# Forgetting attention: exponentials kept in PSUM, reciprocals spread over 128 partitions, four y buffers

## The chip, the cores and the metric

One core of one Trainium2 chip runs one encoder layer for a sequence of 1024 tokens of width 1024. The metric is the device time of one execution in microseconds, lower is better. A core has five engines that run side by side, each through its own instructions in order: PE (TensorE: matmuls; PEld is its weight load), DVE (VectorE), ACT (ScalarE), POOL (GpSimd) and SP (SyncE, which here only issues transfers). PE writes its results to PSUM, a small memory of eight banks of 128 partitions x 512 numbers; everything else lies in SBUF or in DRAM. POOL works on SBUF alone in this kernel.

## The reference, cut to what matters

```python
u = layer_norm(x) * (1 + scale) + shift             # scale, shift, gate from c
h = u @ w_in                                        # split in fq fk fv fg ff | sq sk sv sg
f_cum = cumsum(log_sigmoid(ff + b_f))
# forgetting attention, 8 heads of 64
s = (fq @ fk.T) / 8 + (f_cum[q] - f_cum[k])         # causal: -inf for k > q
y_fox = softmax(s) @ fv * silu(fg)
# stick-breaking attention, 8 heads of 64
y_sb = weights(sq, sk) @ sv * silu(sg)
out = layer_norm(alpha * x + gate * (concat(y_fox, y_sb) @ w_out)) * ln_g + ln_b
```

Every large product is computed in three matmuls: each operand is split in a rounded high part and a rest, and high x high, high x rest and rest x high are summed in PSUM.

## The kernel before, in words

The layer is cut in eight pairs of heads (p = 0 to 7): pairs 0 to 3 are the stick-breaking heads, pairs 4 to 7 the forgetting heads (hh = 0 to 7, p = 4 + hh // 2). The stages follow each other: the normalisation and first projections; the stick-breaking units (`units`, two turns behind them the transposes of `weights_turn`); then the forgetting attention; then the output projection, whose tiles of 128 tokens run in the order 6, 7, 4, 5, 2, 3, 0, 1.

**The order of the work.** PE's instructions stand in the order in which the program writes them (`manual_schedule`, L142 to L143). The other queues are ordered by a planner that simulates times, so a line lower in the program can run earlier there; a queue once ordered is run in order, and an instruction that waits holds what is behind it. The projections of later pairs are "fillers" (L1131): generators of small pieces, a piece about three matmuls of 512 columns, which the loops call between the attention's own work (`fill`, `share`).

**The loop of the forgetting attention** (L1235 to L1265) goes through 96 steps. A step is (head, query group g, key block kb): 128 keys against up to 512 queries. g=1 (the upper 512 queries) has eight key blocks, g=0 four; heads 0 to 5 run g=1 and then g=0, and the last two heads run (6,1), (7,1), (6,0), (7,0). In step n the program writes:

- `fox_scores` of step n (L615): two matmuls (L622, L623) put the scores of keys (partitions) by queries into T, a PSUM tile of two buffers; an additional row of the operands brings minus the row maximum. DVE adds the causal mask on the diagonal block (L625). ACT takes exp of T twice: into SBUF in full (L637, `raw`) and rounded (L638, the high part of `pt`). DVE subtracts the two for the rest (L639); POOL adds `raw` to the sum of the row (L643, in SBUF). After the last key block the sum's two halves of partitions are folded (ACT L646, DVE L647) and split in two parts (ACT L648, DVE L649);
- fillers, and for the groups six steps ahead (`AHEAD`) the maxima: `fox_max` (L588), a matmul into S (one buffer) and a DVE reduction (L600), four times; then `fox_row` (L605), a transpose by PE (L607), a copy by ACT and a transfer on SP's queue into the operand row;
- `fox_pv` of step n-2 (L653): the product with the values, in two PSUM accumulators, one for each half of 256 queries (L665). With a half's last key block, `att_joined` (L528) adds the accumulator's parts into a y buffer `ty` of SBUF (ACT L533, DVE L534 and L535), and the accumulator is free;
- four steps after a group's last score (`NORM_LAG`), `fox_norm` (L670): a matmul with ones spreads the row sum over all partitions into a T buffer (L675), DVE takes the reciprocal of 64 x 512 there (L676), multiplies the gate with it (L677), and `att_gated` (L538) multiplies y with the gate on POOL (L541) and stores it to `y_dr` on SP's queue (L549). For the last pair y stays in SBUF, in two parts (L546, L547).

`ty` has two buffers. From step 80 (`OUT_AT`) a piece of the output projection (L1039 to L1041) follows each step; `load_y` brings the stored y of a token tile back (L1016) and splits it on POOL (L1019, L1020).

Of the kernel before, what the change touches and what calls it, by code (L numbers as in the profile page):

```python
# [14 lines left out]
P = 128  # L15
# [13 lines left out]
def tile_hybrid_layer(  # L29
# [27 lines left out]
    def att_tile(name, dt=F32):  # L57
        return big("att", 6, name, dt)
# [10 lines left out]
    def t_tile(name):  # L69
        return ps.tile([P, 512], F32, tag="T", bufs=2, name=name)  # L70
# [42 lines left out]

    y_dr = dr.tile([NPAIR, P, SEQ], F32, tag="y_dr", name="y_dr")
    wo_dr = dr.tile([2, NPAIR, P, D], F32, tag="wo_dr", name="wo_dr")
    f_dr = dr.tile([3, 8, SEQ], F32, tag="f_dr", name="f_dr")

    def raw_tile(name):
# [404 lines left out]
        summed.append((acc, p, h, j))  # L523

    def att_sum(acc, p, h, j):
        att_gated(att_joined(acc, p, h, j), p, h, j)

    def att_joined(acc, p, h, j):  # L528
        r = slice(h * HD, h * HD + HD)
        o = slice((1 - h) * HD, (1 - h) * HD + HD)  # L530
        ty = sb.tile([P, 512], F32, tag="ty", bufs=2, name=f"ty_{p}_{h}_{j}")
        tm, yt = ty[:, :256], ty[:, 256:]
        nc.scalar.copy(tm[r, :], acc[o, :256])  # L533
        nc.vector.tensor_tensor(yt[r, :], acc[r, :256], tm[r, :], op=ALU.add)  # L534
        nc.vector.tensor_tensor(yt[r, :], acc[r, 256:], yt[r, :], op=ALU.add)  # L535
        return yt
# [17 lines left out]
    def fox_open():  # L554
        QA.append(att_tile("qa_0", F32R))
        wide = fx["wide"] = cp.tile([P, SEQ], BF16, tag="qz", name="wide")
        nc.gpsimd.memset(wide, 0.0)
        nc.gpsimd.affine_select(out=wide[:, SEQ - P:], in_=wide[:, SEQ - P:], pattern=[[-1, P]], base=0,
                                channel_multiplier=1, compare_op=ALU.is_ge, fill=MASKED)
        KA.append(big("kl", 2, "ka_0", F32R))  # L560
        for t in (QA[0], KA[0]):
            nc.gpsimd.memset(t.bitcast(F32)[HD:FK], 1.0)
        fox_load(0)
        tiles = [att_tile(f"fx_{n}") for n in range(3)]
        tiles.append(att_tile("fx_3", F32R))
        parts = [t[:, a:a + 512] for t in tiles for a in (0, 512)]
        fx["raw"], fx["fold"], fx["sum"], fx["hl"] = parts[:3], parts[3][:HD], parts[4:6], parts[6:]
        fx["row"] = parts[3][HD:HD + 4]

    def fox_more():  # L570
        QA.append(att_tile("qa_1", F32R))
# [33 lines left out]
    def fox_row(hh, g):  # L605
        t = s_tile(f"m_{hh}_{g}")[:4, 0, :P]
        nc.tensor.transpose(t, nms.pop((hh, g)), ident)  # L607
        row = fx["row"][:, nrow[0] % 4 * P:][:, :P].bitcast(F32R)
        nrow[0] += 1
        nc.scalar.copy(row, t)  # L610
        nc.sync.dma_start(QA[hh % 2].bitcast(F32)[FM:FK, g * 512:g * 512 + 512], row.bitcast(F32))

    pts, sums, nraw, nsum, hls = {}, {}, [0, 0], [0], {}

    def fox_scores(hh, g, kb):  # L615
        p, h = 4 + hh // 2, hh % 2
        qa, ka = QA[hh % 2], KA[hh % 2]
        q0 = max(0, kb * P - g * 512)
        ks = slice(kb * P, kb * P + P)
        qs = slice(g * 512 + q0, g * 512 + 512)  # L620
        T = t_tile(f"T_{hh}_{g}_{kb}")
        nc.tensor.matmul(T[:, q0:], ka[:FK, ks], qa[:FK, qs], start=True, stop=False)  # L622
        nc.tensor.matmul(T[:, q0:], kst[p][h][:, ks], qst[p][h][:, qs], start=False, stop=True)  # L623
        if kb >= 4 * g:
            nc.vector.tensor_tensor(T[:, q0:q0 + P], T[:, q0:q0 + P], causal, op=ALU.add)  # L625
        if nraw[0] % 2 == 0:
            fx["pt"] = pt_tile(f"pt_{nraw[0]}", F32R, [P, 2, 2, 512])
        pt = pts[hh, g, kb] = fx["pt"][:, nraw[0] % 2]
        nraw[0] += 1
        if kb == 0:  # L630
            raw = sums[hh, g] = fx["sum"][nsum[0] % 2]
            hls[hh, g] = fx["hl"][nsum[0] % 2]
            nsum[0] += 1
        else:
            raw = fx["raw"][nraw[1] % 3]
            nraw[1] += 1
        nc.scalar.activation(raw[:, q0:], T[:, q0:], AF.Exp)  # L637
        nc.scalar.activation(pt[:, 0, q0:], T[:, q0:], AF.Exp)  # L638
        lows[:] = [nc.vector.tensor_tensor(pt[:, 1, q0:], raw[:, q0:], pt.bitcast(F32)[:, 0, q0:], op=ALU.subtract)]  # L639
        if kb:  # L640
            total = sums[hh, g]
            scaled[:] = [*scaled[-3:],
                         nc.gpsimd.tensor_tensor(total[:, q0:], total[:, q0:], raw[:, q0:], op=ALU.add)]  # L643
        if kb == 4 * g + 3:
            total, fold, hl = sums.pop((hh, g)), fx["fold"], hls[hh, g]
            nc.scalar.copy(fold, total[HD:])  # L646
            nc.vector.tensor_tensor(fold, fold, total[:HD], op=ALU.add)  # L647
            nc.scalar.copy(hl[:HD], fold)  # L648
            nc.vector.tensor_tensor(hl[HD:], fold, hl.bitcast(F32)[:HD], op=ALU.subtract)  # L649

    vacc, joined = {}, {}

    def fox_pv(hh, g, kb):  # L653
        p, h = 4 + hh // 2, hh % 2
        pt = pts.pop((hh, g, kb))
        q0 = max(0, kb * P - g * 512)
        for x in range(2):
            if q0 >= 256 * x + 256:
                continue
            if kb == 0:  # L660
                vacc[hh, g, x] = pv_tile(f"pv_{hh}_{g}_{x}", x)
            acc2 = vacc[hh, g, x].rearrange("p (a b) -> p a b", a=2)
            s0 = max(q0 - 256 * x, 0)
            last = kb == 4 * g + 2 * x + 1
            nc.tensor.matmul(acc2[:, :, s0:], vt[p][:, kb, h * P:(h + 1) * P],  # L665
                             pt[:, :, 256 * x + s0:256 * x + 256], start=(kb == 0), stop=last)
            if last:
                joined[hh, g, x] = att_joined(vacc.pop((hh, g, x)), p, h, 2 * g + x)

    def fox_norm(hh, g):  # L670
        p, h = 4 + hh // 2, hh % 2
        r = slice(h * HD, h * HD + HD)
        qs = slice(g * 512, g * 512 + 512)
        l = t_tile(f"l_{hh}_{g}")
        nc.tensor.matmul(l, ones_r.to_broadcast([P, P]), hls.pop((hh, g)), start=True, stop=True)  # L675
        nc.vector.reciprocal(l[r, :], l[r, :])  # L676
        nc.vector.tensor_tensor(sgt[p][r, qs], sgt[p][r, qs], l[r, :], op=ALU.mult)  # L677
        for x in range(2):
            att_gated(joined.pop((hh, g, x)), p, h, 2 * g + x)

# [535 lines left out]
    begin = {}  # L1216
    for n, u in enumerate(steps):
        begin.setdefault(u[:2], n)
    maxima, rows, norms = {}, {}, {}
    for (hh, g), n in begin.items():  # L1220
        for d in range(4):
            maxima[n - AHEAD + d] = (hh, 4 * g + 3 - d)
        rows[n - AHEAD + 4] = (hh, g)
# [106 lines left out]
```

## Time and profile before

| | |
|---|---|
| median of 3 timed runs | 842.82 us (840.62 to 843.74) |
| the profiled execution's own time | 841.72 us |
| its span, first to last instruction | 839.9 us |
| mean granted PE clock | 0.922 |
| busy: PE, DVE, ACT, POOL | 721.0, 606.5, 384.5, 455.8 us |

The profile shows one execution. PE busy time is the union of matmuls that overlap in a pipeline. An idle time is put down to the instruction that released it; "A <- B: t, n, m" in the view of waits says that A waited for B for t us in all, n times, m us at the longest. The granted clock (PEclk) is the share of full speed at which PE may run. L12 is line 12 of the kernel before.

### The profile page before, as it was taken

The page shows a single profiled execution, that of the slowest core. Times are in us where ns is not written, and L with a number is a line of the kernel's source. Part 1 is how long each engine was busy: PE and PEld are TensorE (multiplying, and loading weights), DVE is VectorE, ACT ScalarE, POOL GpSimd, SP SyncE. Part 2 cuts the span into 40 slices and gives each one's busy share as a digit, 9 for nine tenths or more (in the row PEclk, how much of TensorE's full clock was granted, in tenths as well). Part 3 has the DMA queues.
Part 4 walks back from the last instruction along what each step waited for, and adds up shares of the span by engine and source line. Part 5 has one row for each costly group of instructions (what it writes and reads, how often), then busy time and mean ns, then how long its engine had stood idle before and what let it go on. Part 6 is the DMA issues. An engine that isn't in the chain of part 4 may idle for free.

```text
span 839.9 us, 10965 instructions
## 1 busy us (share of the span) xinstructions
PE 721.0 (86%) x3553; PEld 591.5 (70%) x3553; DVE 606.5 (72%) x997; ACT 384.5 (46%) x859; POOL 455.8 (54%) x552
## 2 busy tenths in 40 slices
PE   8999999999999999898767688795866847779996
PEld 5898988899888889776556567674654625557885
DVE  6778797868677686646858777786685777679654
ACT  6574686756767685433523344242352424431000
POOL 6431786646556664786645655647632173356531
PEclk9999999999999999998989889997796777679999
DMA  9945221211122110332313222134123660023411
GB/s 344 398 150 160 70 58 36 64 30 41 51 49 58 36 52 16 98 127 75 100 26 109 74 82 82 57 115 130 57 57 108 219 204 7 0 73 97 170 60 50
DMA packets 45656, 79.63 MB, mean 95 GB/s; under 512 B 5256, under 2 KB 20360, under 8 KB 45600
## 3 DMA queue, kind: packets, MB, share of 16 engines
q1 hardware_dynamic: 45168, 78.67, 29.8%
q8 instruction: 28, 0.46, 0.2%
q10 hardware_dynamic: 432, 0.27, 0.1%
q14 instruction: 28, 0.23, 0.1%
HBM read 56.25 MB, written 16.35 MB: 86 GB/s over the span
## 4 chain that ended last, share of the span: by engine, by line
PE 60%; DVE 19%; issue 7%; ACT 5%; DMA 4%; POOL 4%; SPq 0%; ACTq 0%; POOLq 0%; DVEq 0%
PE m L307 6%; PE m L308 6%; PE m L309 6%; DVE l L676 5%; PE pv L521 4%; PE T L504 4%; DVE pt L639 3%; DVE S L600 3%; PE pv L665 3%; PE o L1039 3%; PE o L1041 3%; PE o L1040 3%; PE v L365 2%; PE v L367 2%; PE v L366 2%
## 5 line engine op out<-in xcount | busy, mean ns | idle before, releaser
L643 POOL TENSOR_TENSOR fx<-fx,fx 128x512 f32<-128x512 f32 (+3 forms) x80 | 82.0, 1025 | 130.6 <-ACT fx L637 85.1
L307 PE MATMUL m<-uh,whi 128*128 128x512 f32 x304 | 128.3, 422 | 0.0
L639 DVE TENSOR_TENSOR pt<-fx,pt 128x512 fp32r<-128x512 f32 (+1 forms) x96 | 91.5, 953 | 50.8 <-ACT pt L638 49.7
L308 PE MATMUL m<-ul,whi 128*128 128x512 f32 x304 | 125.6, 413 | 0.0
L309 PE MATMUL m<-uh,wlo 128*128 128x512 f32 x304 | 125.3, 412 | 0.0
L637 ACT ACTIVATE fx<-T 128x512 f32<-128x512 f32 (+1 forms) x96 | 47.1, 491 | 131.1 <-DVE T L625 92.5
L665 PE MATMUL pv<-pt,v 128*128 128x512 f32 (+1 forms) x160 | 64.3, 460 | 41.8 <-DVE ty L535 40.4
L487 POOL TENSOR_TENSOR be<-be,kp 128x127 f32<-128x127 f32 (+3 forms) x64 | 78.9, 1233 | 35.7 <-DVE kp L485 24.1
L665 PEld LDWEIGHTS pv<-pt,v 128*128 128x128 f32 x160 | 35.1, 229 | 53.5 <-ACT ty L533 31.9
L541 POOL TENSOR_TENSOR ty<-ty,sg 64x256 f32<-64x256 f32 x64 | 50.7, 802 | 38.4 <-DVE sg L677 35.3
L481 DVE TENSOR_TENSOR_SCAN kp<-kp,floor 128x128 f32<-128x128 f32 (+3 forms) x64 | 58.6, 915 | 17.8 <-ACT kp L473 17.5
L309 PEld LDWEIGHTS m<-uh,wlo 128*128 128x128 f32 x304 | 60.7, 200 | 14.9
L307 PEld LDWEIGHTS m<-uh,whi 128*128 128x128 f32 x304 | 61.1, 201 | 11.1 <-issue 0.2
L308 PEld LDWEIGHTS m<-ul,whi 128*128 128x128 f32 x304 | 61.1, 201 | 10.3
L507 DVE TENSOR_TENSOR pt<-T,pt 128x512 fp32r<-128x512 f32 (+2 forms) x96 | 50.7, 550 | 22.4 <-ACT pt L506 21.7
L506 ACT CAST pt<-T 128x512 fp32r<-128x512 f32 (+2 forms) x96 | 44.3, 480 | 37.3 <-PE T L504 36.6
L365 PE MATMUL v<-whi_v,uh 128*128 128x256 f32 (+1 forms) x192 | 56.3, 293 | 3.4 <-DVE v L374 3.4
L676 DVE RECIPROCAL l<-l 64x512 f32<-64x512 f32 x16 | 53.8, 3364 | 7.0 <-PE l L675 6.9
L622 PE MATMUL T<-qa,ka 68*128 68x512 f32 (+1 forms) x96 | 38.1, 397 | 21.9 <-ACT pt L638 9.9
L367 PE MATMUL v<-wlo_v,uh 128*128 128x256 f32 (+1 forms) x192 | 55.6, 290 | 0.0
L366 PE MATMUL v<-whi_v,ul 128*128 128x256 f32 (+1 forms) x192 | 55.5, 289 | 0.0
L600 DVE CUSTOM_DVE_ANT_0 S<-S,wide 128x1024 f32<-128x1024 f32 (+3 forms) x64 | 48.5, 757 | 8.1 <-PE S L595 7.6
(316 smaller groups left out, 1937.6 us busy)
## 6 DMA issues: line engine op xcount, KB each, us to landing
raw<-in_w_qkg_dram SPq DMA_DIRECT2D x38, 256.0 KB
wss<-in_w_ss_dram SPq DMA_DIRECT2D x16, 512.0 KB
x<-in_x_dram SPq DMA_DIRECT2D x8, 512.0 KB
wg<-in_w_gate_dram SPq DMA_DIRECT2D x8, 512.0 KB
raw_o<-in_w_out_dram SPq DMA_DIRECT2D x16, 256.0 KB
wo_dr<-whi_o SPq DMA_DIRECT2D x16, 256.0 KB
wo_dr<-wlo_o SPq DMA_DIRECT2D x16, 256.0 KB
xr<-in_x_dram SPq DMA_DIRECT2D x8, 512.0 KB
```

The costliest lines, as they stand in the source:

```text
L307: nc.tensor.matmul(acc, hi[:, c], u_hi[kt][:, s], start=(kt == 0), stop=False)
L308: nc.tensor.matmul(acc, hi[:, c], u_lo[kt][:, s], start=False, stop=False)
L309: nc.tensor.matmul(acc, lo[:, c], u_hi[kt][:, s], start=False, stop=(kt == NB - 1))
L365: nc.tensor.matmul(acc[:, :n], u_hi[kt][:, ts_], hi[:, s], start=(kt == 0), stop=False)
L366: nc.tensor.matmul(acc[:, :n], u_lo[kt][:, ts_], hi[:, s], start=False, stop=False)
L367: nc.tensor.matmul(acc[:, :n], u_hi[kt][:, ts_], lo[:, s], start=False, stop=(kt == NB - 1))
L487: nc.gpsimd.tensor_tensor(be[:, :ke - 1], be[:, :ke - 1], kp[:, 1:ke], op=ALU.mult)
L600: nc.vector.tensor_tensor_reduce(out=S[:, :ns, :w], in0=S[:, :ns, :w], in1=fx["wide"][:, SEQ - ke:].rearrange("p (a b) -> p a b", a=ns), o ...
L639: lows[:] = [nc.vector.tensor_tensor(pt[:, 1, q0:], raw[:, q0:], pt.bitcast(F32)[:, 0, q0:], op=ALU.subtract)]
L643: nc.gpsimd.tensor_tensor(total[:, q0:], total[:, q0:], raw[:, q0:], op=ALU.add)]
L665: nc.tensor.matmul(acc2[:, :, s0:], vt[p][:, kb, h * P:(h + 1) * P], pt[:, :, 256 * x + s0:256 * x + 256], start=(kb == 0), stop=last)
L676: nc.vector.reciprocal(l[r, :], l[r, :])
```

## The change

1. **Exponentials stay in PSUM.** ACT writes exp of T back to T, and then copies it, rounded, to the high part of `pt`; DVE subtracts T and the high part for the rest, and DVE, no longer POOL, adds T to the row's sum. For the first key block ACT takes a further exp of T straight into the sum. The buffers `raw` are gone.
2. **The fold's add and subtraction** go from DVE to POOL.
3. **Reciprocals by transfers.** A new `fox_sum`, three steps after a group's last score (`SUM_LAG`): the matmul with ones as before; ACT copies one partition of the result (512 numbers) to SBUF; a transfer on ACT's queue spreads them over 128 partitions x 4; DVE takes the reciprocal there; a transfer on SP's queue writes them to a DRAM tile `l_dr`, and a second one reads them back broadcast to 64 partitions (`inv`). `fox_norm` now comes six steps after the last score, and its multiplication of the gate with `inv` is on POOL.
4. **Four y buffers**: the two of `ty` and two in the SBUF that `raw` had; the forgetting heads go round these four.
5. **The transfer of the row of maxima** goes from SP's queue to ACT's.
6. **The opening** of the loop has ten steps in place of eight, with the last two transposes of the stick-breaking units in every second of them, after the fillers; in a step the scores are written first. The maxima of (6,0) and (7,0) come eight and seven steps ahead in place of six.
7. **The output projection** starts at step 84 in place of 80, and the later loads of y move with it; the loop ends two steps later, with the norms.

```diff
-    def att_joined(acc, p, h, j):
+    def att_joined(acc, p, h, j, ty):
...
-        fx["raw"], fx["fold"], fx["sum"], fx["hl"] = parts[:3], parts[3][:HD], parts[4:6], parts[6:]
-        fx["row"] = parts[3][HD:HD + 4]
+        fx["sum"], fx["inv"], fx["fold"], fx["hl"] = parts[0:2], parts[2], parts[3][:HD], parts[6:]
+        fx["row"], fx["l"] = parts[3][HD:HD + 4], parts[3][96:97]
+        fx["ty"] = parts[4:6] + [sb.tile([P, 512], F32, tag="ty", bufs=2, name=f"ty_{n}") for n in range(2)]
...
-        nc.sync.dma_start(QA[hh % 2].bitcast(F32)[FM:FK, g * 512:g * 512 + 512], row.bitcast(F32))
+        nc.scalar.dma_start(QA[hh % 2].bitcast(F32)[FM:FK, g * 512:g * 512 + 512], row.bitcast(F32))
...
+        hi, lo, t = pt[:, 0, q0:], pt[:, 1, q0:], T[:, q0:]
         if kb == 0:
-            raw = sums[hh, g] = fx["sum"][nsum[0] % 2]
-            hls[hh, g] = fx["hl"][nsum[0] % 2]
+            sums[hh, g] = fx["sum"][nsum[0] % 2]
             nsum[0] += 1
-        else:
-            raw = fx["raw"][nraw[1] % 3]
-            nraw[1] += 1
-        nc.scalar.activation(raw[:, q0:], T[:, q0:], AF.Exp)
-        nc.scalar.activation(pt[:, 0, q0:], T[:, q0:], AF.Exp)
-        lows[:] = [nc.vector.tensor_tensor(pt[:, 1, q0:], raw[:, q0:], pt.bitcast(F32)[:, 0, q0:], op=ALU.subtract)]
+            nc.scalar.activation(sums[hh, g], t, AF.Exp)
+        nc.scalar.activation(t, t, AF.Exp)
+        nc.scalar.copy(hi, t)
+        lows[:] = [nc.vector.tensor_tensor(lo, t, pt.bitcast(F32)[:, 0, q0:], op=ALU.subtract)]
+        total = sums[hh, g]
         if kb:
-            total = sums[hh, g]
+            nc.vector.tensor_tensor(total[:, q0:], t, total[:, q0:], op=ALU.add)
+        if kb == 4 * g + 3:
+            fold, hl = fx["fold"], fx["hl"][g]
+            sums.pop((hh, g))
+            nc.scalar.copy(fold, total[HD:])
+            nc.gpsimd.tensor_tensor(fold, fold, total[:HD], op=ALU.add)
+            nc.scalar.copy(hl[:HD], fold)
             scaled[:] = [*scaled[-3:],
-                         nc.gpsimd.tensor_tensor(total[:, q0:], total[:, q0:], raw[:, q0:], op=ALU.add)]
-        if kb == 4 * g + 3:
-            total, fold, hl = sums.pop((hh, g)), fx["fold"], hls[hh, g]
-            nc.scalar.copy(fold, total[HD:])
-            nc.vector.tensor_tensor(fold, fold, total[:HD], op=ALU.add)
-            nc.scalar.copy(hl[:HD], fold)
-            nc.vector.tensor_tensor(hl[HD:], fold, hl.bitcast(F32)[:HD], op=ALU.subtract)
+                         nc.gpsimd.tensor_tensor(hl[HD:], fold, hl.bitcast(F32)[:HD], op=ALU.subtract)]
...
+    def fox_sum(hh, g):
+        l = t_tile(f"l_{hh}_{g}")
+        nc.tensor.matmul(l, ones_r.to_broadcast([P, P]), fx["hl"][g], start=True, stop=True)
+        nc.scalar.copy(fx["l"], l[96:97, :])
+        lp = sb.tile([P, 3, 6], F32, tag="st", bufs=3, name=f"lp_{hh}_{g}")[:, 0, :4]
+        nc.scalar.dma_start(lp, fx["l"])
+        nc.vector.reciprocal(lp, lp)
+        r = slice(hh % 2 * HD, hh % 2 * HD + HD)
+        to = l_dr[hh, g * 512:g * 512 + 512]
+        nc.sync.dma_start(to.rearrange("(p b) -> p b", b=4), lp)
+        nc.sync.dma_start(fx["inv"][r], l_dr[hh:hh + 1, g * 512:g * 512 + 512].to_broadcast([HD, 512]))

     def fox_norm(hh, g):
...
-        l = t_tile(f"l_{hh}_{g}")
-        nc.tensor.matmul(l, ones_r.to_broadcast([P, P]), hls.pop((hh, g)), start=True, stop=True)
-        nc.vector.reciprocal(l[r, :], l[r, :])
-        nc.vector.tensor_tensor(sgt[p][r, qs], sgt[p][r, qs], l[r, :], op=ALU.mult)
+        nc.gpsimd.tensor_tensor(sgt[p][r, qs], sgt[p][r, qs], fx["inv"][r], op=ALU.mult)
...
-    PV_LAG, NORM_LAG, AHEAD = 2, 4, 6
-    OPENING = 8
-    OUT_AT = 80
-    OUT_STEPS = (1, 1, 1, 1, 1, 1, 1, 1, 1, 1, 1, 1, 1, 1, 1, 1, 4)
-    YLOAD = (78, 82, 86, 90, 94)
+    PV_LAG, SUM_LAG, NORM_LAG, AHEAD = 2, 3, 6, 6
+    EARLY = {(6, 0): 8, (7, 0): 7}
+    OPENING = 10
+    OUT_AT = 84
+    OUT_STEPS = (1, 1, 1, 1, 1, 1, 1, 1, 1, 1, 1, 1, 2, 4)
+    YLOAD = (80, 95, 99, 101)
...
-        if n < LAG - OPENING:
-            weights_turn(n + OPENING + len(units))
-        elif n == LAG - OPENING:
+        if 0 <= n < N:
+            fox_scores(*steps[n])
+        fill(share(n + 0.5))
+        if n < 2 * LAG - OPENING and n % 2 == 0:
+            weights_turn((n + OPENING) // 2 + len(units))
+        elif n == 2 * LAG - OPENING:
             weights_turn(len(units) + LAG)
             sum_up()
             fox_more()
-        if 0 <= n < N:
-            fox_scores(*steps[n])
-        fill(share(n + 0.5))
...
+        if n in totals:
+            fox_sum(*totals[n])
```

More of the change, by code (lines that the diff above doesn't have):

```diff
@@ L115, in tile_hybrid_layer @@
     wo_dr = dr.tile([2, NPAIR, P, D], F32, tag="wo_dr", name="wo_dr")
+    l_dr = dr.tile([8, SEQ], F32, tag="l_dr", name="l_dr")
     f_dr = dr.tile([3, 8, SEQ], F32, tag="f_dr", name="f_dr")
@@ L525, in att_sum @@
     def att_sum(acc, p, h, j):
-        att_gated(att_joined(acc, p, h, j), p, h, j)
-    def att_joined(acc, p, h, j):
+        ty = sb.tile([P, 512], F32, tag="ty", bufs=2, name=f"ty_{p}_{h}_{j}")
+        att_gated(att_joined(acc, p, h, j, ty), p, h, j)
+    def att_joined(acc, p, h, j, ty):
         r = slice(h * HD, h * HD + HD)
         o = slice((1 - h) * HD, (1 - h) * HD + HD)
-        ty = sb.tile([P, 512], F32, tag="ty", bufs=2, name=f"ty_{p}_{h}_{j}")
         tm, yt = ty[:, :256], ty[:, 256:]
@@ L563, in fox_open @@
         fox_load(0)
-        tiles = [att_tile(f"fx_{n}") for n in range(3)]
-        tiles.append(att_tile("fx_3", F32R))
+        tiles = [att_tile(f"fx_{n}", F32R if n == 3 else F32) for n in range(4)]
         parts = [t[:, a:a + 512] for t in tiles for a in (0, 512)]
-        fx["raw"], fx["fold"], fx["sum"], fx["hl"] = parts[:3], parts[3][:HD], parts[4:6], parts[6:]
-        fx["row"] = parts[3][HD:HD + 4]
+        fx["sum"], fx["inv"], fx["fold"], fx["hl"] = parts[0:2], parts[2], parts[3][:HD], parts[6:]
+        fx["row"], fx["l"] = parts[3][HD:HD + 4], parts[3][96:97]
+        fx["ty"] = parts[4:6] + [sb.tile([P, 512], F32, tag="ty", bufs=2, name=f"ty_{n}") for n in range(2)]
     def fox_more():
@@ L610, in fox_row @@
         nc.scalar.copy(row, t)
-        nc.sync.dma_start(QA[hh % 2].bitcast(F32)[FM:FK, g * 512:g * 512 + 512], row.bitcast(F32))
-    pts, sums, nraw, nsum, hls = {}, {}, [0, 0], [0], {}
+        nc.scalar.dma_start(QA[hh % 2].bitcast(F32)[FM:FK, g * 512:g * 512 + 512], row.bitcast(F32))
+    pts, sums, nraw, nsum = {}, {}, [0], [0]
     def fox_scores(hh, g, kb):
@@ L667, in fox_pv @@
             if last:
-                joined[hh, g, x] = att_joined(vacc.pop((hh, g, x)), p, h, 2 * g + x)
+                joined[hh, g, x] = att_joined(vacc.pop((hh, g, x)), p, h, 2 * g + x,
+                                                fx["ty"][nty[0] % 4])
+                nty[0] += 1
+    def fox_sum(hh, g):
[9 more added lines that the diff above has]
+        nc.sync.dma_start(fx["inv"][r], l_dr[hh:hh + 1, g * 512:g * 512 + 512].to_broadcast([HD, 512]))
     def fox_norm(hh, g):
@@ L1218, in tile_hybrid_layer @@
         begin.setdefault(u[:2], n)
-    maxima, rows, norms = {}, {}, {}
+    maxima, rows, totals, norms = {}, {}, {}, {}
     for (hh, g), n in begin.items():
+        at = n - EARLY.get((hh, g), AHEAD)
         for d in range(4):
-            maxima[n - AHEAD + d] = (hh, 4 * g + 3 - d)
-        rows[n - AHEAD + 4] = (hh, g)
+            maxima[at + d] = (hh, 4 * g + 3 - d)
+        rows[at + 4] = (hh, g)
+        totals[n + 4 * g + 3 + SUM_LAG] = (hh, g)
         norms[n + 4 * g + 3 + NORM_LAG] = (hh, g)
```

2 lines of the change are left out of this document (1 added, 1 removed).

## The prediction, made before the changed kernel was run

> **What bounds the kernel now.** I began with the first part of the page and a table of stages, cut where the first score matmul of each head of the forgetting attention starts (a head is 12 steps; heads 6 and 7 share one row). A row of the table has the stretch, its length, the busy time of PE, PEld, DVE, ACT and POOL with their instructions, the granted PE clock, the DMA share and GB/s.
>
> ```profile
> span 839.9 us, 10965 instructions
> ...
> 0.00:366.70 366.70, 359.12 (x2050) 306.50 (x2050) 271.16 (x468) 233.68 (x520) 213.42 (x302) 1.00 0.33 102
> 366.70:409.00 42.30, 37.37 (x153) 29.22 (x154) 26.80 (x49) 18.91 (x41) 28.52 (x26) 0.92 0.28 88
> 409.00:462.70 53.70, 37.90 (x151) 28.54 (x150) 39.62 (x59) 19.07 (x42) 30.00 (x31) 0.90 0.27 79
> 462.70:513.00 50.30, 38.97 (x187) 31.49 (x186) 37.88 (x63) 21.65 (x49) 31.39 (x31) 0.86 0.23 71
> 513.00:561.70 48.70, 38.81 (x218) 33.40 (x216) 35.85 (x65) 17.62 (x46) 28.80 (x28) 0.93 0.27 78
> 561.70:616.30 54.60, 41.52 (x155) 32.16 (x154) 38.10 (x59) 19.88 (x43) 32.51 (x34) 0.81 0.33 99
> 616.30:666.10 49.80, 32.90 (x107) 24.21 (x105) 35.28 (x55) 17.74 (x40) 13.92 (x14) 0.74 0.36 117
> 666.10:754.80 88.70, 57.14 (x186) 42.67 (x185) 65.09 (x101) 32.19 (x73) 41.29 (x44) 0.74 0.27 89
> 754.80:839.90 85.10, 77.27 (x357) 63.28 (x355) 56.70 (x83) 3.79 (x9) 35.96 (x44) 0.99 0.27 93
> ```
>
> The first and last rows have PE nearly full at full clock: little to win there. The 388.1 us between them are the stage of the change. PE is busy for 284.6 us of them, so it idles 103.5; DVE is busy 278.6 (72%), POOL 206, ACT 147. No engine is full: the stage is bound by waits. A second loss is the clock: length times (1 - PEclk), row by row, is 3.4 + 5.4 + 7.0 + 3.4 + 10.4 + 12.9 + 23.1 = 65.6 us of withheld clock.
>
> The waits of that window name what PE stood for:
>
> ```profile
> PE pv L665 <- DVE ty L535: 40.4, 11, 6.9
> PE m L607 <- DVE nm L600: 19.5, 12, 3.6
> PE S L595 <- DVE nm L600: 18.3, 18, 3.5
> PE T L622 <- ACT pt L638: 9.9, 6, 3.0
> PE T L622 <- DVE sg L677: 6.5, 3, 3.2
> ```
>
> Three groups: the product with the values (L665) waits for its accumulator to be summed into a y buffer; the row of maxima and the maxima (L607, L595) wait for DVE; the scores (L622) wait for a T buffer. Smaller ones bring the sum to the 103.5. One of the long stalls, in order of time:
>
> ```profile
> 566.82 0.62 POOL L130 TENSOR_SCALAR whi<-raw 128x512 fp32r<-128x512 f32 x1 [4.13 <-DMA raw<-in_w_qkg_dram]
> ...
> 571.96 1.15 SPq L549 DMA_DIRECT2D y_dr<-ty  x2
> ...
> 574.69 0.36 ACT L533 COPY ty<-pv 64x256 f32<-64x256 f32 x1 [0.37 <-DMA y_dr<-ty]
> ...
> 576.00 1.19 PE L665 MATMUL pv<-pt,v 128*128 128x512 f32 x2 [6.60 <-DVE ty L535]
> ```
>
> With two y buffers, the joined output of (head, g=0) cannot be written until that of (head, g=1) was normalised (reciprocal, L677), gated on POOL (L541) and stored; POOL itself had stood for a weight load. PE then stood 6.60 us. The clock around it, in stretches of 3.4 us:
>
> ```profile
> 568.20:571.60 3.40, 1.19 (x6) 0.64 (x4) 3.31 (x4) 0.21 (x1) 3.32 (x3) 1.00 0.85 271
> 571.60:575.00 3.40, 0.00 (x0) 0.00 (x0) 0.96 (x3) 0.68 (x2) 3.32 (x4) 0.51 0.19 40
> 575.00:578.40 3.40, 2.40 (x6) 2.00 (x7) 1.11 (x3) 0.31 (x2) 3.31 (x5) 0.50 0.20 77
> 578.40:581.80 3.40, 3.40 (x10) 2.73 (x9) 2.10 (x3) 0.83 (x2) 2.45 (x4) 0.50 0.75 231
> 581.80:585.20 3.40, 3.40 (x16) 2.79 (x16) 2.35 (x1) 0.37 (x1) 1.24 (x1) 0.98 0.24 73
> ```
>
> After a mostly idle stretch the grant is half; it comes back after a full one. In the three half-clock stretches PE was busy 5.8 of 10.2 us, so about 0.6 of the 65.6 is felt: 40 us, or 0.39 us per us of idle.
>
> **The change, part by part.** (a) *Four y buffers.* The y wait, 40.4 us. Two of the four hold g=1 until its norm while g=0 fills the others; these are wanted again six steps after the g=1 norm. What stays between L665 and its accumulator is one copy and two adds, about 1.2 us, against a step of over 3 us. Late next is DVE's queue. Bounds: 30 to 40 gone; I take 37, as no other row names the buffer.
>
> (b) *DVE.* The rows:
>
> ```profile
> L639 DVE TENSOR_TENSOR pt<-fx,pt 128x512 fp32r<-128x512 f32 (+1 forms) x96 | 91.5, 953 | 50.8 <-ACT pt L638 49.7
> L507 DVE TENSOR_TENSOR pt<-T,pt 128x512 fp32r<-128x512 f32 (+2 forms) x96 | 50.7, 550 | 22.4 <-ACT pt L506 21.7
> L676 DVE RECIPROCAL l<-l 64x512 f32<-64x512 f32 x16 | 53.8, 3364 | 7.0 <-PE l L675 6.9
> ...
> L507 DVE TENSOR_TENSOR pt<-T,pt 128x512 fp32r<-128x512 f32 x48 | 32.1, 682 | 14.1 <-ACT pt L506 13.7
> ...
> L649 DVE TENSOR_TENSOR fx<-fx,fx 64x512 fp32r<-64x512 f32 x16 | 12.6, 786 | 0.5
> L647 DVE TENSOR_TENSOR fx<-fx,fx 64x512 f32<-64x512 f32 x16 | 12.2, 763 | 3.4 <-ACT fx L646 3.3
> ...
> L677 DVE TENSOR_TENSOR sg<-sg,l 64x512 f32<-64x512 f32 x15 | 10.2, 680 | 0.3
> ...
> 683.35 0.69 DVE L639 TENSOR_TENSOR pt<-fx,pt 128x512 fp32r<-128x512 f32 x1 [3.07 <-ACT pt L638]
> ```
>
> Away go reciprocals (53.8), multiplies and folds (10.2 + 12.2 + 12.6): 88.8. The 96 subtractions read T in PSUM as L507 does, in the same shapes: 96 x 0.550 = 52.8 in place of 91.5. New are 80 sums, the same less 16 full ones: 52.8 - 16 x 0.682 = 41.9. The reciprocal of 4 elements is, by 3364/512 ns each, 0.03 us and a start; at most 0.2, so 3 in all. Net -88.8 - 38.7 + 41.9 + 3 = -83: DVE falls from 278.6 to about 196. L607 and L595 wait (37.8 us) because a 3.36 us block stands in DVE's queue while the row of the next group is due. Bounds: nothing (the late ops are others) to all; I take two thirds, 25, nearest to the block's size.
>
> The Trainium skill (VectorE: DVE Perf Modes, section on the TRN2 errata) speaks against this part: a VectorE operation from PSUM has 62 cycles more fixed cost than one from SBUF, which would be 65 ns on 176 operations, 11 us more on DVE. Here an undisturbed subtraction of 512 from SBUF takes 0.69 us and one from PSUM 0.682, so the trace doesn't bear it out; by the page the term would be 22 in place of 25.
>
> (c) *T held longer.* T was free after L638; now after subtraction and sum, 2 x 0.68 us more. With two buffers that shows only where the sum of the row (L675) takes one between two steps: 16 times, 0.68 more on average, +11. On the other side the 6.5 us behind L677 go, since that buffer is now freed by a copy. Bounds -6 to +22; I take +4.4.
>
> (d) *The row sum comes a step earlier and through POOL.*
>
> ```profile
> L646 ACT COPY fx<-fx 64x512 f32<-64x512 f32 x16 | 9.9, 618 | 6.5 <-POOL fx L643 6.4
> ...
> L131 POOL TENSOR_TENSOR wlo_o<-raw_o,whi_o 128x512 fp32r<-128x512 f32 x14 | 18.2, 1299 | 0.2
> L643 POOL TENSOR_TENSOR fx<-fx,fx 128x512 f32<-128x512 f32 (+3 forms) x80 | 82.0, 1025 | 130.6 <-ACT fx L637 85.1 <-DVE pt L639 30.5 <-ACT v L373 5.6
> ```
>
> Copy, add, cast, subtract: 2 x 0.62 + 2 x 1.30 = 3.8 us after the last sum, due three steps (some 10 us) later. POOL loses 82 us of sums and gets 48 operations of 1.30, 62: 206 to 186 of a shorter stage. Behind a weight wait such as the 4.13 us above, L675 would stand, and PE with it, as its order is written out. Bounds 0 to 16 x 3 = 48; I take 6, two bad groups.
>
> (e) *Reciprocals by transfers.* What the trace has of such transfers, from the chain, and of SP's queue:
>
> ```profile
> 572.64 1.97 DMA y_dr<-ty
> 673.87 4.49 DMA y_dr<-ty
> ...
> SPq L549 <- POOL ty L541: 161.6, 43, 13.8
> ```
>
> Copy, three landings, a reciprocal: 0.6 + 3 x 1.97 + 0.2 = 6.7 us at the quick row, 14.3 at the slow one, within three steps (some 10 us) before POOL's multiply. Cost zero at the quick row, and covered for the y buffers by the six steps. Uncovered, POOL stands 4 us per group. Queues: ACT gets 32 issues (0.58 us by L549's row, two in 1.15), 16 copies and 16 first exps, some 40 us on 147 of 388, hidden; behind an issue wait the exps and L533. DVE waits for the landing of each 128x4, with subtractions and maxima behind it: bounds 0 to 16 x 1.97 = 32, inside (b)'s. SP waits for a DVE result and then a landing, with stores of y and weight loads behind; it stood 161.6 us for L541 alone without PE missing a weight, so zero.
>
> (f) *Opening, early maxima, output.* The longer opening moves filler matmuls ahead, and later steps get less: zero, bounds -3 to +3. By n=95 12 output steps are done in place of 16; a step is three matmuls, and the row below (88 in 20 us) makes that 4 x 0.68 = 2.7 us more at the end.
>
> ```profile
> 780.00:800.00 20.00, 20.00 (x88) 1.00 0.48 159
> ```
>
> The sum: idle -37 - 25 + 4.4 + 6 = -51.6; clock 0.39 x 51.6 = -20, one more as the longest waits go: -21; end +2.7. In all -70. The profiled execution took 841.7 us (span 839.9, 1.8 around it), 1.1 below the median of 842.8: 771.7 on its own, 773 on the median; I say 772.
>
> **The rivals.**
> A: *the clock stays full.* If what is left are waits of 1 to 2 us, no stretch gets mostly idle, and all 40 us of felt clock come back: 772 - 19 = 753; with DVE's lateness wholly gone (12.8 of idle and the 5 of clock inside the 40), 740. For it: head 4's four-step group, which has no long stall, ran at full clock:
>
> ```profile
> 603.30:616.30 13.00, 11.34 (x55) 9.09 (x54) 11.31 (x24) 8.12 (x19) 3.58 (x5) 1.00 0.12 25
> ```
>
> Against: heads 6 and 7 have few filler matmuls, and their PE is busy 64% now. The Trainium skill (TensorE: Matmul & The Clock Gate, Part 1) asks for an idle window of 3.4 us before the clock halves, which would make this the likelier case; here a stretch with PE busy 1.19 of 3.40 us was enough, so I don't follow it.
> B: *only the y wait goes.* DVE's 25 us stay, since its ops are fewer but the maxima still queue: idle -26.6, clock -10, end +2.7: 809.
> C: *slower: POOL's queue waits for the transfers.* The normalising multiply stands at the head of POOL's in-order queue until three landings are through; the folds of the next group are behind it, and the row sum on PE behind them. It decides when a group's chain (3.8 + 14.3) outlasts the distance between sums, 4 steps or 13 us in g=0. To cancel the 70 us it takes 70/1.39/16 = 3.1 us of PE per group; at the slow row's 5 us over: 16 x 5 x 1.39 = 111, so 772 + 111 = 883. For it: the 4.49 us landing. Against: the 1.97 us one, and that SP's long waits cost PE nothing so far.
> D: *no change:* DVE's order keeps L533 late for other reasons: 843.
>
> **How the numbers follow.** Forecast 0.54, A 0.18, B 0.16, C 0.08, D 0.04. The first three are faster: 0.88; D same: 0.04 (within 0.5%, about what a measurement here can tell); C 0.08. The range reaches well into A and B, 733 to 820, leaving out D, C and their far ends, under 0.2.
>
> **What will show it.** (a) right: L665 hardly waits for L535; (b) right: L607 and L595 wait under 13 us; (c) L622 waits for the sum; (d) wrong if L675 waits for POOL; (e) wrong if the multiply waits for the broadcast and the folds are late behind it; clock: PEclk over 0.9 in heads 1 to 4. If the eight-step groups still take over 35 us, the forecast fails.

## The result, and the profile after

The changed kernel takes 802.92 us (median of 4 runs, 802.19 to 809.46; the kernel before beside it 842.58, 840.62 to 843.74): a ratio of 0.955, 95% interval 0.950 to 0.960. That is 40 us less, where 70 were forecast; inside the range, and nearest to rival B (809). In one run each of `psum_y4` and `all_three` below, the granted clock was 0.55 and the time 1168 and 1124 us, and their medians leave it out.

First the table by stage, cut as before at the first score matmul of each head; columns as in the prediction.

```profile
0.00:368.90 368.90, 363.05 (x2063) 310.09 (x2064) 271.17 (x468) 233.43 (x520) 215.47 (x305) 1.00 0.32 102
368.90:408.00 39.10, 34.24 (x148) 26.91 (x147) 24.50 (x55) 21.03 (x44) 15.67 (x15) 0.96 0.28 84
408.00:449.90 41.90, 36.07 (x151) 27.21 (x150) 25.60 (x61) 20.95 (x45) 30.54 (x31) 0.96 0.40 111
449.90:499.60 49.70, 38.95 (x194) 32.63 (x193) 28.15 (x71) 25.17 (x57) 30.64 (x31) 0.90 0.39 112
499.60:539.30 39.70, 34.91 (x211) 30.25 (x210) 25.45 (x67) 19.31 (x49) 25.71 (x26) 1.00 0.31 99
539.30:579.50 40.20, 33.41 (x149) 25.79 (x148) 25.77 (x60) 21.45 (x45) 21.61 (x22) 1.00 0.37 101
579.50:621.50 42.00, 28.80 (x101) 21.12 (x99) 24.46 (x59) 20.37 (x44) 10.46 (x10) 0.80 0.35 109
621.50:707.00 85.50, 58.77 (x178) 42.45 (x178) 41.41 (x106) 38.03 (x84) 32.02 (x34) 0.72 0.40 112
707.00:801.00 94.00, 81.93 (x369) 66.43 (x368) 50.83 (x83) 4.62 (x10) 42.26 (x50) 0.96 0.28 92
```

Against the rows of before: heads 0 to 4 went from 249.6 to 210.6 us, head 5 from 49.8 to 42.0, heads 6 and 7 only from 88.7 to 85.5; the opening grew by 2.2 and the end by 8.9. In the stage between (388.1, now 338.1 us) PE is busy 265.1 us, so it idles 73.0 in place of 103.5. DVE is busy 195.3 us, the forecast's 196, and the withheld clock, worked out row by row as before, is 40.6 us in place of 65.6.

The waits of that stage (window 360 to 730 us). In the new numbering L596 is the maxima, L608 the transpose of the row, L623 the scores, L665 the product with the values, L674 the spread of the row sum, L678 the reciprocal, L688 the normalising multiply:

```profile
POOL sg L688 <- DMA fx<-l_dr: 41.6, 12, 11.1
...
DVE lp L678 <- DMA lp<-fx: 31.7, 11, 7.3
...
PE S L596 <- DVE nm L601: 21.6, 15, 4.0
...
PE m L608 <- DVE nm L601: 17.5, 11, 2.8
...
PE l L674 <- POOL fx L649: 8.1, 4, 3.7
...
PE T L623 <- DVE pt L638: 7.5, 3, 5.8
...
PE T L623 <- DMA qa<-fx: 6.2, 2, 3.3
PE T L623 <- DVE fx L641: 6.2, 7, 2.2
...
PE pv L665 <- ACT pt L637: 2.6, 1, 2.6
...
PE pv L665 <- DVE ty L536: 1.3, 1, 1.3
```

Of the wait of 40.4 us for the y buffer 1.3 are left. The two for the maxima are still 39.1 us (before 37.8), though DVE lost 83 us of work. New are 31.7 us that DVE stands for a transfer, and 41.6 us that POOL stands for the broadcast.

The groups of the changed lines (busy time, mean ns of one | idle before it and its releaser):

```profile
L638 DVE TENSOR_TENSOR pt<-T,pt 128x512 fp32r<-128x512 f32 (+1 forms) x96 | 53.2, 556 | 55.7 <-ACT pt L637 55.0
...
L641 DVE TENSOR_TENSOR fx<-T,fx 128x512 f32<-128x512 f32 (+3 forms) x80 | 41.7, 521 | 0.0
...
L678 DVE RECIPROCAL lp<-lp 128x4 f32<-128x4 f32 x16 | 2.8, 176 | 31.7 <-DMA lp<-fx 31.7
```

The work itself costs what was forecast: 53.2 for 52.8 us, 41.7 for 41.9, 2.8 for 3. What the forecast had wrong is who waits for whom.

One of the transfers in heads 6 and 7, in order of time (SPq and ACTq issue transfers; a bracket gives the idle time before an instruction and its releaser), and its pieces in the chain that ended last:

```profile
619.91 0.32 SPq L1000 DMA_DIRECT2D wol<-wo_dr  x1
...
620.33 0.38 SPq L999 DMA_DIRECT2D woh<-wo_dr  x1
...
621.46 0.56 ACTq L677 DMA_DIRECT2D lp<-fx  x1
...
630.52 0.18 DVE L678 RECIPROCAL lp<-lp 128x4 f32<-128x4 f32 x1 [7.28 <-DMA lp<-fx]
...
631.33 0.79 PE L623 MATMUL T<-qa,ka 68*128 68x512 f32 x1 [5.80 <-DVE pt L638]
```

```profile
621.46 9.04 DMA lp<-fx
...
632.35 6.64 DMA fx<-l_dr
```

The 2 KB of row sums landed after 9.04 us. Two loads of 512 KB of the output weights had been issued 1.5 and 1.1 us ahead on SP's queue. DVE stood 7.28 us in its order for the row sums; its next subtraction, which reads T, came behind that, and PE's scores waited 5.80 us for this T. The broadcast then took 6.64 us more.

### The profile page after: what moved, and what is told of

The parts are those of the page before. It is cut to its first block, busy times and chain, and to the rows that moved or that the text cites. A ratio compares the mean times of both kernels' runs of the same rounds, so it can differ in the third digit from the quotient of the medians.

```text
span 801.0 us, 11015 instructions
## 1 busy us (share of the span) xinstructions
PE 710.1 (89%) x3553; PEld 582.9 (73%) x3553; DVE 517.3 (65%) x1029; ACT 404.4 (50%) x891; POOL 424.4 (53%) x520
## 5 line engine op out<-in xcount | busy, mean ns | idle before, releaser
L308 PE MATMUL m<-uh,whi 128*128 128x512 f32 x304 | 126.0, 414 | 0.0
L309 PE MATMUL m<-ul,whi 128*128 128x512 f32 x304 | 123.6, 407 | 0.0
L310 PE MATMUL m<-uh,wlo 128*128 128x512 f32 x304 | 123.5, 406 | 0.0
L638 DVE TENSOR_TENSOR pt<-T,pt 128x512 fp32r<-128x512 f32 (+1 forms) x96 | 53.2, 556 | 55.7 <-ACT pt L637 55.0
L636 ACT ACTIVATE T<-T 128x512 f32<-128x512 f32 (+1 forms) x96 | 45.7, 476 | 68.5 <-DVE T L626 54.1
L482 DVE TENSOR_TENSOR_SCAN kp<-kp,floor 128x128 f32<-128x128 f32 (+3 forms) x64 | 58.6, 915 | 17.8 <-ACT kp L474 17.5
L665 PE MATMUL pv<-pt,v 128*128 128x512 f32 (+1 forms) x160 | 58.6, 430 | 5.4 <-ACT pt L637 2.6
L507 ACT CAST pt<-T 128x512 fp32r<-128x512 f32 (+2 forms) x96 | 44.2, 480 | 35.8 <-PE T L505 35.2
L646 POOL TENSOR_TENSOR fx<-fx,fx 64x512 f32<-64x512 f32 x16 | 20.5, 1280 | 75.9 <-ACT fx L645 63.6
L623 PE MATMUL T<-qa,ka 68*128 68x512 f32 (+1 forms) x96 | 38.3, 398 | 20.7 <-DVE pt L638 7.5
L474 ACT ACTIVATE kp<-S 128x384 f32<-128x384 f32 (+4 forms) x96 | 44.0, 494 | 21.9 <-PE S L468 20.7
L596 PE MATMUL S<-ka,qa 67*128 67x512 f32 (+4 forms) x96 | 33.0, 400 | 22.5 <-DVE nm L601 21.6
L1050 PE MATMUL o<-woh,whi_y 128*128 128x512 f32 (+1 forms) x119 | 47.7, 401 | 3.8 <-DVE r L1069 3.8
```

Source lines behind the costliest of these rows:

```text
L308: nc.tensor.matmul(acc, hi[:, c], u_hi[kt][:, s], start=(kt == 0), stop=False)
L309: nc.tensor.matmul(acc, hi[:, c], u_lo[kt][:, s], start=False, stop=False)
L310: nc.tensor.matmul(acc, lo[:, c], u_hi[kt][:, s], start=False, stop=(kt == NB - 1))
L482: last_dve = nc.vector.tensor_tensor_scan(rv, rv, floor[:, :ke - lo], initial=0.0, op0=ALU.mult, op1=ALU.max)
L638: lows[:] = [nc.vector.tensor_tensor(lo, t, pt.bitcast(F32)[:, 0, q0:], op=ALU.subtract)]
L1050: nc.tensor.matmul(acc, yh, hi[:, s], start=(pr == 0), stop=False)
```

## The experiments

Three questions. Can the gains of the y buffers and of DVE's shorter queue be added up? What do the transfers cost? Whose wait are the 39 us at the maxima? Ratios are against runs of the kernel before on the same chip (840.3 to 841.4 us).

**The parts alone.** `psum_only` is the kernel before with exp in PSUM and the sums on DVE; `psum_y4` has four y buffers as well.

```diff
-        nc.scalar.activation(raw[:, q0:], T[:, q0:], AF.Exp)
-        nc.scalar.activation(pt[:, 0, q0:], T[:, q0:], AF.Exp)
+        nc.scalar.activation(t, t, AF.Exp)
+        nc.scalar.copy(hi, t)
...
-                         nc.gpsimd.tensor_tensor(total[:, q0:], total[:, q0:], raw[:, q0:], op=ALU.add)]
+            nc.vector.tensor_tensor(total[:, q0:], t, total[:, q0:], op=ALU.add)
...
+        fx["ty"] = parts[:2] + [sb.tile([P, 512], F32, tag="ty", bufs=2, name=f"ty_{n}") for n in range(2)]
```

(The last line is `psum_y4`'s alone.)

> The kernel before with part 1 alone: exponentials in PSUM and the sums on DVE; two y buffers, folds on DVE, reciprocals in PSUM, order and opening as before. DVE's work by the prediction: -38.7 + 41.9, so no change from that, and T held 1.4 us longer, which the 40 us wait for the joining covers: 838 to 846. If the longer hold shows beside it, 846 to 860; if POOL, freed of 82 us of sums, brings the gated y earlier, 825 to 838.

> The kernel before with the exponentials in PSUM, the sums on DVE and four y buffers; folds on DVE, reciprocals in PSUM, norm four steps behind, opening and output as before. DVE's work is as before (-38.7 + 41.9). Both theories: PE's wait for L535 falls from 40.4 us to under 6. If the y buffers bring what the prediction gave them (37 us of idle and 14 of clock), 790 to 800; if another wait takes their place in the same steps, 815 to 835.

Measured: 836.13 us, 0.994 (0.992 to 0.997), and 836.08 us, 0.993 (0.991 to 0.996). On top of the exponentials the four buffers bring nothing. PE's waits for T and y, first of `psum_only`, then of `psum_y4`:

```profile
PE T L622 <- DVE pt L638: 18.9, 7, 4.8
...
PE T L622 <- DVE sg L675: 16.8, 7, 3.5
...
PE pv L663 <- DVE ty L535: 10.2, 9, 2.7
```

```profile
PE T L623 <- DVE pt L639: 23.1, 7, 5.4
...
PE T L623 <- DVE sg L678: 14.0, 6, 3.2
...
PE T L623 <- DVE fx L642: 8.2, 4, 4.8
...
PE pv L664 <- DVE ty L535: 2.2, 2, 1.9
```

With the sums off POOL, which gates y (L541), the y wait is 10.2 us in place of 40.4, without a buffer more. Whether that is because POOL gates y sooner, or because PE, held at T, now comes to the y buffer later, these two runs don't separate. T itself is now read by DVE until the row's sum is made. DVE's queue still holds the 3.36 us reciprocals with their multiply (L675 here, L678 below), and the scores wait for T behind them and behind the subtractions: 36 us in these rows, 40 with the 4.5 behind the sum, and 45 with four buffers; in the kernel before it was 16.4 in the rows of the prediction. One wait took the place of the other.

`y4_only` is the kernel before with each y buffer cut in halves, the scratch copy of a joining in the next half.

```diff
+        fx["ty"] = [t[:, a:a + 256] for t in ty for a in (0, 256)]
...
+                                                fx["ty"][(nty[0] + 1) % 4], fx["ty"][nty[0] % 4])
```

> The kernel before with four y buffers alone (the two tiles cut in four halves, the copy of ACT in the half that is free). PE's wait for L535 falls from 40.4 us to under 6. The prediction's step (a): 37 us of idle and 14 of clock go, 788 to 800. Rival (the T buffers take its place: with PE no longer held at L665 it arrives a few us later at a T buffer that the reciprocal of 64x512 still holds): PE's waits for L677 and L638 grow from 16 us to over 35, 822 to 840.

Measured: 838.12 us, 0.997 (0.993 to 1.001). It isn't the test it was meant to be, since the scratch goes into a half that is still being stored:

```profile
PE pv L666 <- DVE ty L534: 37.9, 10, 8.4
...
ACT ty L532 <- DMA y_dr<-ty: 18.9, 4, 7.2
```

What four whole buffers do in the kernel before was not measured.

**One part undone.** `recip_psum` is the changed kernel with the old reciprocal in the new place, `y2` the changed kernel with two y buffers.

```diff
-        nc.vector.reciprocal(lp, lp)
+        nc.vector.reciprocal(l[r, :], l[r, :])
+        nc.vector.tensor_tensor(sgt[p][r, qs], sgt[p][r, qs], l[r, :], op=ALU.mult)
```

```diff
-                                                fx["ty"][nty[0] % 4])
+                ty = sb.tile([P, 512], F32, tag="ty", bufs=2, name=f"ty_{hh}_{g}_{x}")
+                joined[hh, g, x] = att_joined(vacc.pop((hh, g, x)), p, h, 2 * g + x, ty)
```

> The changed kernel with part 3 undone: DVE takes the reciprocal of 64x512 in PSUM again (3.36 us) and multiplies the gate (0.68), in the step of the row sum; y is gated three steps later as in the changed kernel. 65 us of DVE work come back, no transfer is left. Theory 1: blocks and landings cost PE about the same, 795 to 812. Theory 2: DVE's work decides, and 62 us more of it cost at least 25 us of PE: 828 or more.

> The changed kernel with two y buffers in place of four, taken in turn as before; nothing else undone. With the norm six steps behind, a y buffer of g=1 is stored later than before. Step (a) of the prediction: PE's wait at the value products for the joining comes back, 40 us or more and its clock: 850 to 880. Rival (the y buffers bring nothing, as the cut halves seemed to say): 800 to 810.

Measured: 830.32 us, 0.986 (0.982 to 0.990), and 844.48 us, 1.006 (1.002 to 1.010). With everything else of the change in place, transfers with two y buffers make a kernel no faster than before, four y buffers with the old reciprocal one that is 11 us faster, and both together 40. The waits of `y2` say why:

```profile
POOL sg L686 <- DMA fx<-l_dr: 71.9, 11, 12.9
...
PE pv L664 <- DVE ty L536: 51.9, 9, 11.0
```

POOL's stand for the broadcast holds the gating of y, and with two buffers PE stands behind it. This is rival C's mechanism, reaching PE by the y buffers. Four buffers keep it from PE.

What the old reciprocal costs, `recip_psum` shows in PE's waits for T:

```profile
PE T L623 <- DVE fx L641: 20.0, 12, 3.7
PE T L623 <- issue: 18.8, 7, 4.4
```

In the second row the profile names no releaser; each of the seven times the scores start about 0.1 us after the end of the multiply (L679) that follows a reciprocal, and both of these read a T buffer. So the move of the reciprocal pays by the T buffers, 38.8 us here beside 13.7 in the changed kernel. The waits at the maxima are 44.2 us beside 39.1.

**What the transfers cost.** `no_inv` leaves the division by the row sum out: no copy, no transfers, no reciprocal, no multiply. `late_recip` writes the reciprocal and SP's two transfers two steps later, behind that step's subtraction. `lnexp` takes 1/l as exp(-ln l) on ACT, without transfers.

```diff
-        nc.vector.reciprocal(lp, lp)
+        fx["lp"] = lp
...
+        if n - INV_LATER in totals:
+            fox_inv(*totals[n - INV_LATER])
```

```diff
+        nc.scalar.activation(fx["inv"][r], l[r, :], AF.Ln)
+        nc.scalar.activation(fx["inv"][r], fx["inv"][r], AF.Exp, scale=-1.0)
```

(The first diff is `late_recip`, the second `lnexp`.)

> The changed kernel without its reciprocal chain: the row sum's matmul stays, but the copy of its row, the three transfers, the 128x4 reciprocal and POOL's multiplication are left out, so y is not divided by the row sum. Theory 1 (landings: DVE's 31.7 us and POOL's 41.6 us of standing for transfers hold back the maxima, the T buffers and the folds): the two waits vanish, PE's wait for L601 falls from 39 us to under 20, and the time is 765 to 780. Theory 2 (DVE's own work is what the maxima wait for; the landings only fill idle time): 793 to 803.

> The changed kernel with the 128x4 reciprocal and the two transfers behind it issued two steps later, on DVE behind that step's subtraction; nothing else changed. Theory 1: DVE's wait for the first landing falls from 31.7 us to under 8, PE's wait for L601 falls by 10 to 20, POOL's wait for the broadcast grows by up to two steps a group; 780 to 795. Theory 2: the wait on DVE goes as well but PE's wait for L601 stays, 798 to 806. Slower than 806 if POOL's wait is what decides.

> The changed kernel with the reciprocal of the row sum by ACT as exp(-ln(l)), 64x512 from PSUM into the buffer inv: no transfer, no work on DVE, 1.2 us more of ACT a group and whatever its function tables cost. Theory 1 (landings): DVE's and POOL's waits for them are gone, 780 to 788, as without the reciprocals (782) and POOL's 20 us more. If ACT has to load tables twice a group, 16 x 2.6 = 41 us of ACT come to it, ahead of the exponentials: 800 to 825.

Measured: `no_inv` 782.03 us, 0.930 (0.927 to 0.933); `late_recip` 795.00, 0.945 (0.942 to 0.949); `lnexp` 794.68, 0.944 (0.941 to 0.947). So the reciprocals still cost some 21 us in the changed kernel, and 8 of these go when DVE takes the result up later (its wait falls from 31.7 to 4.7 us). Heads 6 and 7 of `no_inv`:

```profile
616.30:686.40 70.10, 52.01 (x178) 38.15 (x177) 42.45 (x106) 36.62 (x83) 29.43 (x34) 0.77 0.39 123
```

They take 70.1 us in place of 85.5: 15.4 of the 21 lie there. `lnexp` has no transfer either, yet gains 8 us and not 21. Beyond `no_inv` it has POOL's multiplications, two more operations of ACT a group, and table loads of ACT, which are likely the larger part:

```profile
L676 ACT ACT_TABLE_LOAD x16 | 20.5, 1283 | 1.4 <-ACT fx L611 0.6 <-ACT pt L637 0.5
```

With those ahead of other lines they are 33, 42 us of ACT (33 x 1.283); one of them is in the changed kernel too. The Trainium skill (ScalarE: Activation LUTs, section on table sets) lists one set that holds both exp and ln, so that going from one to the other should need no second load; the program as built here loads at each change.

In all three the waits at the maxima stay. So neither theory of the expectations fits: the time goes down as in the first, the waits stay as in the second. Those of `no_inv`, where no reciprocal and no landing is left on DVE:

```profile
PE S L596 <- DVE nm L601: 21.3, 16, 3.6
PE m L608 <- DVE nm L601: 19.5, 13, 3.0
```

That ends the prediction's reading that the reciprocal block is behind them.

**Whose wait the maxima are.** Two places of the changed kernel, in order of time:

```profile
430.11 1.23 DVE L601 CUSTOM_DVE_ANT_0 S<-S,wide 128x1024 f32<-128x1024 f32 x1 [0.23 <-PE S L596]
...
431.45 0.27 PE L608 MATMUL m<-ident,nm 128*4 128x128 f32 x1 [1.38 <-DVE nm L601]
...
488.21 0.69 DVE L638 TENSOR_TENSOR pt<-T,pt 128x512 fp32r<-128x512 f32 x1 [0.19 <-ACT pt L637]
488.82 0.95 DVE L601 CUSTOM_DVE_ANT_0 S<-S,wide 128x768 f32<-128x768 f32 x1
...
489.89 0.59 PE L596 MATMUL S<-ka,qa 67*128 67x320 f32 x2 [3.61 <-DVE nm L601]
```

In the first place the step writes new maxima (1024 wide, 1.23 us on DVE) ahead of the transpose of the finished row; both use the one S buffer, so the transpose waits for a reduction made a moment ago. In the second the reduction is ordered behind the subtraction of its own step (`with after(*lows)` in `fox_max`), which has scores, exp and rounding ahead of it; the next maxima wait 3.61 us for S. In both places DVE itself had stood idle just before (0.23 and 0.19 us), so these two have nothing to do with its load. `row_first` writes the row ahead of the maxima; `max_early` orders the reduction behind the subtraction of the step before.

```diff
-        if n in maxima:
-            fox_max(*maxima[n])
         if n in rows:
             fox_row(*rows[n])
+        if n in maxima:
+            fox_max(*maxima[n])
```

```diff
-        with after(*lows):
+        with after(*lows_before):
...
+        lows_before[:] = lows
```

> The changed kernel with the row of maxima (transpose L608) written ahead of the maxima in a step that has both. They share the one S buffer, so as it is the transpose stands behind the 1.2 us reduction of the maximum written just ahead of it. Theory 3 (the order in the S buffer makes PE wait, not DVE's load): PE's wait at the transpose falls from 17.5 us to under 5 and the time by 10 to 25, to 778 to 793. Theory 2 (DVE is late by its load): the wait moves to the next maximum, 798 to 806.

> The changed kernel with the reductions of the maxima held on DVE behind the subtraction of the step before, in place of that of their own step (which needs the step's matmuls, mask, exp and cast first). Theory 3: PE's wait for L601 at the next maxima matmul falls from 21.6 us to under 10, 785 to 796. Theory 2: the subtractions come later instead and the value products wait, 799 to 812.

Measured: 790.30 us, 0.939 (0.936 to 0.942), and 772.58 us, 0.919 (0.915 to 0.922). The waits of `row_first`, then of `max_early`:

```profile
PE S L596 <- DVE nm L601: 24.5, 20, 3.5
...
PE m L608 <- DVE nm L601: 8.0, 7, 2.8
```

```profile
DVE lp L680 <- DMA lp<-fx: 25.9, 14, 4.8
...
PE m L609 <- DVE nm L602: 10.1, 9, 1.8
...
PE S L597 <- DVE nm L602: 2.3, 2, 2.1
```

The first edit takes half of the transpose's wait (17.5 to 8.0, where under 5 was expected), and the maxima's grows by 3. The second takes nearly all of the maxima's (21.6 to 2.3) and some of the transpose's, and the time follows: 30 us for one changed dependence, more than expected, while DVE still stands 25.9 us for landings.

`before_order` puts both orders into the kernel before.

> The kernel before with the two orders alone: the row of maxima ahead of the maxima in a step that has both, and the reductions behind the subtraction of the step before. Theory 3 (these waits are a matter of order in the S buffer and on DVE, and have nothing to do with the reciprocals): PE's 37.8 us at L595 and L607 fall below 20, 815 to 830. Theory 2 (they come from DVE's blocks): the waits stay over 30, 835 to 843.

Measured: 816.52 us, 0.973 (0.969 to 0.977).

```profile
PE pv L667 <- DVE ty L536: 47.7, 12, 7.8
...
PE S L596 <- ACT fx L611: 7.9, 7, 3.0
...
PE m L608 <- DVE nm L601: 3.3, 4, 1.3
```

The 37.8 us were a matter of order before the change too: 3.3 are left, with 7.9 for the copy of the row, the 3.36 us reciprocals still on DVE. The y wait grew from 40.4 to 47.7.

**All three.** `all_three` is the changed kernel with both orders and the late reciprocal.

> The changed kernel with the two orders and the reciprocals two steps later. If the three take away different waits, 802.9 - 30.3 - 12.6 - 7.9 = 752, so 748 to 760; if they take away the same one, 765 to 774.

Measured: 766.46 us, 0.913 (0.908 to 0.918), the lowest median here; the interval overlaps that of `max_early`.

```profile
368.80:667.10 298.30, 250.92 (x1125) 198.56 (x1123) 194.80 (x481) 167.24 (x362) 162.91 (x162) 0.91 0.40 119
```

The stage takes 298.3 us, with 47.4 of idle. The gains don't add: 30 + 13 + 8 off 803 would be 752. Most of it is `max_early`'s.

## Why the prediction was right and wrong

The ledger of the spans: PE's idle in the stage fell by 30.5 us (forecast 51.6). PE's busy time there fell by 19.5; the stage has some 25 matmuls fewer (1157 to 1132; 13 more stand in the opening, 12 at the end), 6.1 us at its mean of 284.6/1157, so 13.4 are put down to the clock (forecast 21). The opening is 2.2 longer (0), the end 8.9 (2.7). Together -38.9. The 31 us between 772 and 803 are thus 21 of idle, 8 of clock less 6 of matmuls that moved, and 8 at the two ends. That 803 lies in the range is no merit of the sum: the range was drawn to reach into rival B.

(a) **Four y buffers: right by its row, wrong as a term.** L665 stood 2.6 us for another reason and 1.3 for a y buffer: the y wait fell by 39.1, for 37. But the step "no other row names the buffer" took the row as the price of the buffers alone. In `psum_only` most of that wait goes without a buffer more, and other waits replace it; `psum_y4` gains nothing from the buffers; with the transfers they are worth 42 us (`y2` to the changed kernel). The buffers and the transfers each lay behind the other, and neither had a price of its own.

(b) **DVE: the load right, the wait wrong.** This is the step that failed: "because a 3.36 us block stands in DVE's queue". DVE's busy time came out within 1 us, and the waits rose by 1.3 us where 25 were to go. `no_inv` keeps them without any reciprocal, `max_early` (12.4 us left) and `before_order` (3.3, and 7.9 behind ACT) take most of them away with a changed order. What held the maxima was the one S buffer and the order put in by hand. The price put on them was of the right size: 25 of idle and 10 of clock was forecast, `max_early` gained 30. That the reciprocal left DVE did pay, 27 us between `recip_psum` and the changed kernel, but mostly at the T buffers, a place that (c) priced only at the 6.5 us behind L677. The condition set in the prediction, L607 and L595 under 13 us, did tell it apart. The rule of the Trainium skill that it weighed (VectorE: DVE Perf Modes, section on the TRN2 errata), 65 ns more for an operation from PSUM, isn't seen: the subtraction at 488.21 took 0.69 us from PSUM, as the one from SBUF in the prediction.

(c) **T held longer.** The waits for T behind DVE and ACT went from 16.4 to 13.7 in the rows shown, -2.7 for +4.4, inside its bounds. That the reciprocal leaves DVE is what keeps it small; without that they are 45 us in `psum_y4` and 38.8 in `recip_psum`. Part 5, costed at nothing, has its row too: the scores' waits for the row of maxima (L622, now L623, behind qa<-fx) were 2.3 us before and are 6.2 now.

(d) **Row sum by POOL.** 8.1 us in 4 waits, for 6 in two groups: right.

(e) **Transfers at zero: wrong.** Of the two rows, 1.97 and 4.49 us, the quick one was taken; landings ran up to 9.04. The bound of 32 us for DVE standing was met almost exactly (31.7), by luck, since it is 11 waits of up to 7.3 us and not 16 of 1.97; and it was counted as inside (b). `no_inv` puts the whole of part 3's remaining cost at 21 us, 15 of them in heads 6 and 7. These gained only 3.2 us, and 18.6 without the transfers. That POOL stands (41.6 us) cost PE little by its own rows, the 8.1 us of (d).

(f) **Opening and end.** 12 matmuls more at the end (357 to 369) are the 2.7 forecast. Of the other 6.2 us, 4.3 are idle (7.8 to 12.1) and 2 a lower grant (0.99 to 0.96). `recip_psum` and `y2`, with the same output steps behind a longer stage, have ends of 88.9 and 88.7 us with 7.5 and 7.9 of idle. So it isn't the steps alone; nor is it the transfers, for `no_inv` has 94.0 us with 10.4 of idle. The wait that grew is that of PE's output product (L1050) for DVE's L1069, from 0.7 to 3.8 us; what makes it longer was not tested. Nor was the opening.

**The clock** followed the idle: 13.4 us for 30.5, 0.44 us per us where 0.39 was read. Heads 3 and 4 ran at full clock, head 2 at 0.90, heads 6 and 7 at 0.72. Of the tests set, a grant over 0.9 in heads 1 to 4 was met but for head 2, and eight-step groups under 35 us were met (25 to 33); neither looked at heads 6 and 7 and the end, which gave 3.2 us and took 8.9. Rival A, a clock that stays full, is out, and would be without most of the waits at the maxima too: the whole stage has a grant of 0.88, that of `max_early` 0.90, that of `all_three` 0.91.

**The rivals.** B, "only the y wait goes", comes nearest in time and in what stayed: the maxima still wait. In part that is luck: B has them queue on DVE, which isn't why, and has nothing for the longer opening and end. Nor was DVE's shorter queue worth nothing: without the reciprocal's move the kernel takes 830. C exists as a wait of POOL and decides only with two y buffers, 844. D is out.

## What to carry to other kernels

A wait for an engine is not yet a wait for that engine's load: before a lighter queue is priced, look at what the awaited instruction was itself held for (a buffer just written, an order put in by hand). Two waits that can stand behind each other have one price together, not two; each edit alone may then show nothing, as 836 and 844 us did beside 803. A result that travels through DMA should be asked for late, because the instruction that takes it up holds everything behind it in its queue: two steps later was worth 8 us here.

## What was not expected of the hardware

A transfer of 2 KB took 9.04 us to land with two 512 KB loads issued 1.5 and 1.1 us ahead of it, on another engine's queue, and more loads of that queue close behind. The kernel before has transfers of 2 KB in its chain too, those of the row of maxima (qa<-fx), and they took 2.03 and 1.69 us; the prediction's quick row of 1.97 was a store of 64 KB. The Trainium skill (DMA: Bandwidth & Descriptors, section Issuing engines are not separate DMA queues) says that transfers run on the same 16 engines and interleave, whichever engine started them; these 9.04 us are in keeping with it. That the loads are the cause was seen in the order of time, not tried by moving them.
